# One of four weight sums of a Strassen-like gate/up unit, made by a load and an adding transfer instead of by GpSimd

## The chip, the cores and the metric

The kernel runs on one core of one Trainium2 chip. A core has TensorE (PE in the profile; PEld is its weight load), VectorE (DVE), ScalarE (ACT), GpSimd (POOL) and SyncE (SP), which here only issues DMA transfers. The metric is the device time of one execution in microseconds; runs of before and after are compared on the same chip.

## The reference, cut to what matters

The program is a decoder trunk of two layers on 512 tokens of width 1024, float32. Each layer has two SwiGLU FFNs with a mixer between them. The change touches the FFNs alone:

```python
def swiglu(h, w_gate, w_up, w_down):
    return (jax.nn.silu(h @ w_gate) * (h @ w_up)) @ w_down

for l in range(DEPTH):                       # 2
    x = x + 0.5 * swiglu(rms_norm(x, ffn1_norm[l]), ffn1_w_gate[l], ffn1_w_up[l], ffn1_w_down[l])
    ...                                      # mixer: convolution and differential attention
    x = x + 0.5 * swiglu(rms_norm(x, ffn2_norm[l]), ffn2_w_gate[l], ffn2_w_up[l], ffn2_w_down[l])
```

`w_gate` and `w_up` are 1024 x 2816, `w_down` is 2816 x 1024.

## The kernel before, in words

**Layout and precision.** Features lie on the 128 partitions, tokens along the row. D_FF is cut into 22 tiles of 128. Each float32 operand of a matmul is split in two float32r parts: a high part by a ScalarE copy and a low part, the operand less its high part, by VectorE. A product is then three matmuls (high x high, high x low, low x high).

**An FFN.** `ffn` does its first 5 feature tiles plainly (`PLAIN`), with three matmuls of 512 columns per step. The other 17 run as *units* in two parts, `PARTS[1:]`: 8 gate/up units and 4 Down units, then 9 gate/up units and 4 Down units. A gate/up unit makes the gate and the up product of one feature tile together as a 2 x 2 block product: two halves of the features by two halves of the tokens. With a Winograd form it needs seven half products in place of eight. Each half product is 4 steps of 3 matmuls of 256 columns, so a unit has 84 matmuls (L378, `product`).

**The weights of a unit.** With u1, u2 the first and second half of the up weights (128x512 each) and g1, g2 those of gate, the seven products need seven weight blocks. Four raw tiles hold them:

- A: u1 + u2, then u2 (A is the loaded up tile, its first half overwritten by the sum)
- B: g1, g2 (the loaded gate tile)
- C: g1 + u1 + u2, then g1 + g2 + u1 + u2
- D: g1 + u1, 128x512

`GateUp.load` (L456 on) loads u and g through SP's queue (L458, L459: 512 KB each), and `Unit.sums` makes the four sums on GpSimd: D (L355), A (L356) and the two halves of C (L357, L358). Then each of the four tiles is split by `hi` (ScalarE, L364) and `lo` (VectorE, L368).

**Buffers.** The raw tiles A, B and C come from a ring of 5 (`wraw`), D from a ring of one (`wraw2`). The high and low parts have rings of 4 for A, B, C and of 2 for D (`whi2`, `wlo2`). The two rings of 2 are used once more: by the two halves of the third plain tile of the first FFN (`by_halves`).

**The order of the work.** `Unit.body` writes the order of one unit: its products, the copies of partial sums out of PSUM (`keep`: L396, L407, L427), the finishing of the unit before, and the splits for the next unit. The matmuls that begin a half product are held in program order (L380). All other instructions are placed by a scheduler that simulates the program: it may move an instruction ahead on its engine as soon as what it needs is there, and each engine then runs its list strictly in order. In the body the order is: product with A (u1 + u2), copy `keep[3]` (L396), A of the next unit split, product with u2, B of the next unit's high part, the product with D of the unit *before* (`rest`), product with g1, copy `keep[:2]` (L407), D of the next unit split, product with g2, C of the next unit split, the two products with C, and copy `keep[2]` (L427).

**Neighbours.** In the mixer and at the ends of an FFN, `Prep` makes the next stage's operands: high part (L226, ScalarE), low part (L227, VectorE), square (L235, ScalarE) and its running sum on GpSimd (L239). TensorE transposes that sum (L196) and VectorE and GpSimd (L189) make the norm of each row from it. The Down units (`Down.load`, loads at L512) use the same `sums` with the same rings and keep it in the change.

Of the kernel before, what the change touches and what calls it, by code (L numbers as in the profile page):

```python
# [15 lines left out]
ALU = mybir.AluOpType  # L16
# [52 lines left out]
def trunk(ctx: ExitStack, tc: tile.TileContext, xt, par, lamv, relb, onehot,  # L69
          gu1, dn1, wag, wqkv, wout, gu2, dn2, out):  # L70
    nc = tc.nc
    V, S, G, T = nc.vector, nc.scalar, nc.gpsimd, nc.tensor
# [20 lines left out]
    def ring(tag, n=1024):  # L93
        dt = F32 if "raw" in tag else F32R
        return wp.tile([P, n], dt, tag=tag, name=tag, bufs=RING[tag])
# [70 lines left out]
    for k0, k1 in ((0, 1), (1, 4), (4, KT)):  # L166
        h = slice(k0 * P, k1 * P)
# [281 lines left out]
    class GateUp(Unit):  # L449
# [6 lines left out]
        def load(self):  # L456
            u, g = ring("wraw"), ring("wraw")
            nc.sync.dma_start(u, self.src[1])  # L458
            nc.sync.dma_start(g, self.src[0])  # L459
            d, more = ring("wraw2", 512), ring("wraw")  # L460
            h = slice(0, 512), slice(512, 1024)
            self.sums(u[:, h[0]], u[:, h[1]], g[:, h[0]], g[:, h[1]], d, more[:, h[0]], more[:, h[1]])
            self.raw = {"A": u, "B": g, "C": more, "D": d}
            self.cols = {k: n for k, (_, n) in self.WIDE.items()}

# [754 lines left out]
```

## Time and profile before

| what | us |
|---|---|
| median of 3 runs | 1781.65 |
| lowest, highest run | 1780.59, 1783.45 |
| the profiled execution, its own time | 1779.9 |
| its span in the profile | 1778.1 |
| GpSimd's D sums (L355): 68 of 128x512 in gate/up units | 95.2 busy |
| DMA traffic over the span | 177.87 MB, 100 GB/s |

The profile is of one execution. A row of the timeline reads: start, duration (us), engine, line, operation, written tile <- read tiles, shape; in brackets, how long the engine was idle before it and who released it. In a table of stretches, each engine has its busy time and its number of instructions. In the list of DMA issues the last number is the median time from the issue to the landing. The tile names `wraw`, `whi`, `wlo` stand for all rings, with D's among them: a 128x512 split at L364 or L368 is D's.

### The profile page before, as it was taken

How to read it: one execution, taken by the hardware profiler on the slowest of the kernel's cores; microseconds unless marked ns; L12 is line 12 of the kernel's file. 1: busy time of each engine (PE TensorE's matmuls, PEld its weight loads, DVE VectorE, ACT ScalarE, POOL GpSimd, SP SyncE). 2: the span in 40 equal slices, each digit the busy share in tenths (PEclk: the TensorE clock that was granted, in tenths of full speed). 3: DMA queues.
4: the chain of work that ended last, by engine and by line, in shares of the span. 5: the costliest groups of instructions: out<-in, count | busy, mean ns of one | idle time of the engine just before them, and what ended most of it. 6: DMA issues, size and time to landing. Idle time of an engine off the chain costs nothing.

```text
span 1778.1 us, 30234 instructions
## 1 busy us (share of the span) xinstructions
PE 1765.5 (99%) x11725; PEld 1617.3 (91%) x11725; DVE 1394.3 (78%) x1997; ACT 986.9 (56%) x1579; POOL 965.4 (54%) x665
## 2 busy tenths in 40 slices
PE   9999999999999999999999999999999999999999
PEld 7899999988788899999988999999877888999998
DVE  6978787868857978788767887877788588787875
ACT  6456565645844456466534664665558354564663
POOL 2276566379952156566303655653898433565661
PEclk9999999999999999999999999999999999999999
DMA  6233333423122223333332333334230232333332
GB/s 225 96 113 96 107 107 105 144 85 96 47 72 83 83 95 107 107 98 118 118 95 72 108 96 108 106 102 148 72 119 25 72 107 73 106 96 108 107 105 75
DMA packets 74225, 177.87 MB, mean 100 GB/s; under 512 B 8951, under 2 KB 30726, under 8 KB 74080
## 3 DMA queue, kind: packets, MB, share of 16 engines
q1 hardware_dynamic: 72480, 174.10, 31.1%
q8 instruction: 92, 1.51, 0.3%
q0 software_dynamic: 1312, 1.67, 0.3%
q14 instruction: 53, 0.43, 0.1%
q10 hardware_dynamic: 288, 0.16, 0.0%
HBM read 173.79 MB, written 3.42 MB: 100 GB/s over the span
## 4 chain that ended last, share of the span: by engine, by line
PE 89%; DVE 6%; issue 2%; POOL 2%; ACT 1%; DMA 0%; DVEq 0%; SPq 0%; ACTq 0%
PE ps_pair L378 48%; PE ps_pair L141 5%; PE ps_pair L142 5%; PE ps_pair L138 5%; PE ps_d L378 3%; DVE wlo L368 2%; PE ps_d L141 2%; PE ps_d L142 2%; PE ps_d L138 2%; PE ps_sc L990 2%; PE ps_pair L867 2%; PE ps_pair L868 2%; PE ps_pair L866 2%; PE ps_out L138 1%; PE ps_out L142 1%
## 5 line engine op out<-in xcount | busy, mean ns | idle before, releaser
L368 DVE TENSOR_TENSOR wlo<-wraw,whi 128x1024 fp32r<-128x1024 f32 (+4 forms) x400 | 510.3, 1277 | 171.9 <-ACT whi L364 171.4
L364 ACT ACTIVATE whi<-wraw 128x1024 fp32r<-128x1024 f32 (+4 forms) x400 | 373.6, 935 | 333.5 <-PE ps_pair L378 153.1
L355 POOL TENSOR_TENSOR wraw<-wraw 128x512 f32<-128x512 f32 (+1 forms) x100 | 127.8, 1278 | 554.7 <-DVE wlo L368 366.5
L378 PE MATMUL ps_pair<-acth,wlo 128*128 128x256 f32 x1088 | 307.9, 283 | 0.0
L378 PE MATMUL ps_pair<-actl,whi 128*128 128x256 f32 x1088 | 307.9, 283 | 0.0
L378 PE MATMUL ps_pair<-acth,whi 128*128 128x256 f32 x1088 | 307.9, 283 | 0.0
L378 PE MATMUL ps_pair<-th,whi 128*128 128x256 f32 x816 | 231.8, 284 | 1.2 <-ACT keep L427 0.4
L378 PE MATMUL ps_pair<-tl,whi 128*128 128x256 f32 x816 | 230.9, 283 | 0.0
L378 PE MATMUL ps_pair<-th,wlo 128*128 128x256 f32 x816 | 230.9, 283 | 0.0
L378 PEld LDWEIGHTS ps_pair<-actl,whi 128*128 128x128 f32 x1088 | 208.9, 192 | 0.2
L378 PEld LDWEIGHTS ps_pair<-acth,whi 128*128 128x128 f32 x1088 | 208.9, 192 | 0.2
L378 PEld LDWEIGHTS ps_pair<-acth,wlo 128*128 128x128 f32 x1088 | 208.9, 192 | 0.0
L101 ACT ACTIVATE whi<-wraw 128x1024 fp32r<-128x1024 f32 (+3 forms) x124 | 123.2, 1000 | 150.5 <-PE ps_pair L141 84.3
L141 PE MATMUL ps_pair<-actl,whi 128*128 128x512 f32 x448 | 174.6, 390 | 0.6 <-DVE actl L227 0.5
L142 PE MATMUL ps_pair<-acth,wlo 128*128 128x512 f32 x448 | 174.2, 390 | 0.0
L138 PE MATMUL ps_pair<-acth,whi 128*128 128x512 f32 x448 | 173.6, 393 | 0.1
L357 POOL TENSOR_TENSOR wraw<-wraw 128x512 f32<-128x512 f32 (+1 forms) x100 | 169.3, 1693 | 7.9
L358 POOL TENSOR_TENSOR wraw<-wraw 128x512 f32<-128x512 f32 (+1 forms) x100 | 164.3, 1643 | 7.8
L378 PEld LDWEIGHTS ps_pair<-th,whi 128*128 128x128 f32 x816 | 156.6, 192 | 3.1 <-ACT keep L427 3.1
L378 PEld LDWEIGHTS ps_pair<-th,wlo 128*128 128x128 f32 x816 | 156.6, 192 | 0.0
L378 PEld LDWEIGHTS ps_pair<-tl,whi 128*128 128x128 f32 x816 | 156.6, 192 | 0.0
L356 POOL TENSOR_TENSOR wraw<-wraw 128x512 f32<-128x512 f32 (+1 forms) x100 | 149.9, 1499 | 7.6
(203 smaller groups left out, 4402.1 us busy)
## 6 DMA issues: line engine op xcount, KB each, us to landing
wraw<-in_gu SPq DMA_DIRECT2D x172, 512.0 KB, 3.5
wraw<-in_wqkv SPq DMA_DIRECT2D x24, 512.0 KB, 3.5
wraw<-in_wag SPq DMA_DIRECT2D x16, 512.0 KB, 3.6
wraw<-in_wout SPq DMA_DIRECT2D x16, 512.0 KB, 3.5
wraw<-in_dn SPq DMA_DIRECT2D x60, 128.0 KB, 3.1
wraw<-in_dn SPq DMA_DIRECT2D x20, 384.0 KB, 3.2
wraw<-in_dn SPq DMA_DIRECT2D x28, 256.0 KB, 3.1
wraw<-in_dn SPq DMA_DIRECT2D x20, 320.0 KB, 3.5
```

The source lines that it names most:

```text
L101: S.activation(hi, raw, AF.Copy)
L138: first = T.matmul(ps, wh, xh, start=start, stop=False)
L141: T.matmul(ps, wh, xl, start=False, stop=False)
L142: T.matmul(ps, wl, xh, start=False, stop=stop)
L355: G.tensor_tensor(d, g1, u1, op=ALU.add)
L356: G.tensor_tensor(u1, u1, u2, op=ALU.add)
L357: G.tensor_tensor(m0, u1, g1, op=ALU.add)
L358: G.tensor_tensor(m1, m0, g2, op=ALU.add)
L364: pinned(S.activation(hi[:, : self.cols[k]], self.raw[k][:, : self.cols[k]], AF.Copy), pin)
L368: pinned(V.tensor_tensor(out=lo[:, :c], in0=self.raw[k][:, :c], in1=f32(hi[:, :c]), op=ALU.subtract), pin)
L378: mm = T.matmul(ps, l, r, start=first and i == n == 0, stop=False, skip_group_check=True)
L866: T.matmul(ps[n], xh[:, t], wh, start=k == 0, stop=False)
```

## The change

In `GateUp.load`, D is no longer summed on GpSimd. SP loads the first half of the gate weights into D's buffer, GpSimd does the three other sums, and GpSimd's DMA queue issues a transfer that adds the first half of the up weights, read from HBM once more, to D's buffer.

```diff
@@ -459,7 +459,11 @@
             nc.sync.dma_start(g, self.src[0])
             d, more = ring("wraw2", 512), ring("wraw")
             h = slice(0, 512), slice(512, 1024)
-            self.sums(u[:, h[0]], u[:, h[1]], g[:, h[0]], g[:, h[1]], d, more[:, h[0]], more[:, h[1]])
+            nc.sync.dma_start(d, self.src[0][:, h[0]])
+            G.tensor_tensor(u[:, h[0]], u[:, h[0]], u[:, h[1]], op=ALU.add)
+            G.tensor_tensor(more[:, h[0]], u[:, h[0]], g[:, h[0]], op=ALU.add)
+            G.tensor_tensor(more[:, h[1]], more[:, h[0]], g[:, h[1]], op=ALU.add)
+            nc.gpsimd.dma_start(d, self.src[1][:, h[0]], accum_op=ALU.add)
             self.raw = {"A": u, "B": g, "C": more, "D": d}
             self.cols = {k: n for k, (_, n) in self.WIDE.items()}
```

In the changed kernel the new lines are L462 (load of D), L463 (A sum), L464 and L465 (C sums) and L466 (adding transfer); every line behind them has a number higher by 4. Both transfers of a unit move 128 rows of 2 KB (256 KB).

## The prediction

> **What bounds the kernel now.** I read the page first (shares of the engines, then the chain), then the table of stretches, then TensorE's own waits, and last one gate/up unit in order of time.
>
> ```profile
> span 1778.1 us, 30234 instructions
> ...
> PE 1765.5 (99%) x11725; PEld 1617.3 (91%) x11725; DVE 1394.3 (78%) x1997; ACT 986.9 (56%) x1579; POOL 965.4 (54%) x665
> ...
> PE 89%; DVE 6%; issue 2%; POOL 2%; ACT 1%; DMA 0%; DVEq 0%; SPq 0%; ACTq 0%
> ```
>
> TensorE (PE) is busy in all but 12.6 us (1778.1 less 1765.5), and the chain runs along it. A change on GpSimd (POOL) can win no more than its share of these 12.6 us; it can lose any amount by making TensorE wait.
>
> ```profile
> 133.00:177.00 44.00, 44.00 (x369) 44.00 (x368) 38.15 (x55) 27.44 (x46) 27.24 (x19) 1.00 0.32 97
> ...
> 488.00:533.00 45.00, 42.66 (x255) 36.23 (x254) 24.73 (x73) 20.97 (x57) 26.07 (x20) 1.00 0.23 71
> ...
> 1733.00:1778.00 45.00, 40.75 (x275) 37.58 (x273) 23.55 (x30) 13.58 (x20) 6.97 (x6) 0.99 0.22 74
> ```
>
> Columns: stretch, length, then busy us of PE, PEld, DVE, ACT, POOL. The idle time lies at the end (4.3 us) and in the mixers (2.3 us in the second row). Among the units PE is full: 369 matmuls in 44 us are 0.119 us each, so a gate/up unit with 84 of them (7 products, 4 steps, 3 matmuls) lasts **10.0 us**. Of PE's waits only this one belongs to the units:
>
> ```profile
> PEld ps_pair L378 <- ACT keep L427: 3.1, 9, 0.6
> ```
>
> It comes about once in each of the eight unit parts. Here it is, with the neighbours that matter below, engine by engine:
>
> ```profile
> 126.50 0.33 SPq L458 DMA_DIRECT2D wraw<-in_gu  x1
> ...
> 126.62 0.68 DVE L368 TENSOR_TENSOR wlo<-wraw,whi 128x512 fp32r<-128x512 f32 x1
> ...
> 127.38 1.29 POOL L355 TENSOR_TENSOR wraw<-wraw 128x512 f32<-128x512 f32 x1 [5.10 <-DVE wlo L368]
> 128.75 2.16 POOL L356 TENSOR_TENSOR wraw<-wraw 128x512 f32<-128x512 f32 x1
> ...
> 130.94 1.06 ACT L364 ACTIVATE whi<-wraw 128x1024 fp32r<-128x1024 f32 x1 [1.94 <-POOL wraw L356]
> 131.91 0.36 ACT L427 ACTIVATE keep<-ps_pair 128x256 f32<-128x256 f32 x1
> ...
> 134.51 0.62 ACT L364 ACTIVATE whi<-wraw 128x512 fp32r<-128x512 f32 x1
> 135.50 0.60 ACT L407 ACTIVATE keep<-ps_pair 128x512 f32<-128x512 f32 x1 [0.37 <-PE ps_pair L378]
> ...
> 132.32 0.39 PE L378 MATMUL ps_pair<-th,whi 128*128 128x256 f32 x1
> ...
> 138.18 0.28 PE L378 MATMUL ps_pair<-th,whi 128*128 128x256 f32 x1
> ```
>
> D's low part of one unit ends at 127.30, which frees the only D buffer. GpSimd's sum for the next D follows, then its A sum (L356) to 130.91; the high part of A waits for it; the copy L427 stands behind that on ScalarE (ACT) until 132.27, and PE's next product begins at 132.32, some 0.3 us late.
>
> **The change part by part.** *Removed:* 68 sums of D on GpSimd (17 gate/up units in each of 4 FFNs), 1.3 us each in the row above. Because the A sum then waits for no D buffer, the high part of A can move ahead, and the wait for L427 goes: at most 3.1 us for nine, and as the ninth may lie elsewhere I take 8 x 0.3 = **-2.4 us**. What is late next is PE itself, so the rest of the 68 x 1.3 us is worth nothing. The Down units keep their four sums.
>
> *Added:* 68 loads of 256 KB on SP's queue and 68 adding transfers from GpSimd. In the order in which the changed kernel's instructions stand, D is no longer tied to its unit's sums. SP has, in the steady part, A of unit n+1, D of n, B of n+1; GpSimd has the A sum of n+1, the adding transfer for D of n, the two C sums of n+1. ScalarE and VectorE keep their order, apart from the first two D splits of each FFN, which come far earlier (below). The load waits until D of n-1 is split; so D becomes a ring of one buffer: load, add, high part, low part, next load. If one turn is longer than 10.0 us, it sets the pace of the gate/up units.
>
> ```profile
> wraw<-in_gu SPq DMA_DIRECT2D x172, 512.0 KB, 3.5
> ...
> wraw<-in_dn SPq DMA_DIRECT2D x60, 128.0 KB, 3.1
> ...
> wraw<-in_dn SPq DMA_DIRECT2D x28, 256.0 KB, 3.1
> ...
> d<-d POOLq DMA_DIRECT2D x1, 1280.0 KB, 19.3
> ...
> lamv<-in_lamv POOLq DMA_DIRECT2D x2, 128.0 KB, 3.2
> ...
> oneh<-in_onehot POOLq DMA_DIRECT2D x1, 66.0 KB, 4.4
> ```
>
> The turn without the add: the load is between the 256 KB and the 512 KB row, 3.3 us, since the A load was issued just ahead; four handovers of 0.08 us (127.30 to 127.38) are 0.3; high part 0.6, low part 0.7. Together 4.9 us, so 10.0 - 4.9 = **5.1 us remain for the add**, from issue to landing. The trace has no adding transfer. The bounds are GpSimd's own transfers: 3.2 us for half the bytes and no second read, and 19.3 us for five times the bytes between two places in HBM. I take **4.5 us**, nearest to the 3.2 us row: doubled bytes and the second read of D are each a doubling, worth 0 to 0.4 us by SP's three rows, and the B load beside it shares the DMA engines, for which I add the rest (the 66 KB row took 4.4 us, more than its bytes explain). So one turn is 9.4 us and fits, with 0.6 us to spare.
>
> There is a deadline inside the unit. ScalarE stands in order: the high part of D (134.51), then L407, whose copy PE needs before 138.18. L407 lasts 0.60, the high part 0.62, so D must land by about 136.9 or PE waits. D's load issued at 127.4 lands at 130.7; the A sum must end first (A's load of 126.50 lands at 130.0, the sum takes 1.3 to 2.2 us, to 131.4 to 132.2); the add lands 4.5 us later, **135.9 to 136.8**. In time, by 0.1 to 1.0 us. Then VectorE's low part is at most 2 us later than now; PE uses D only in the rest product of the following unit, and that begins (132.32 for the unit before) a whole unit later. SP's B load stands behind D's load, but waited for a later split (C) anyway; the C sums wait behind the add's issue on GpSimd, some 0.6 us in place of 1.3. These I cost at nothing; their cover is the 10 us of the unit.
>
> The transfer's issue needs GpSimd itself:
>
> ```profile
> 29.95 2.48 DVE L102 TENSOR_TENSOR wlo<-wraw,whi 128x1024 fp32r<-128x1024 f32 x2
> ...
> 31.29 0.59 POOL L764 DMA_DIRECT2D oneh<-in_onehot  x1
> ```
>
> An issue in the middle of VectorE's splits took 0.59 us, as elsewhere. The Trainium skill (SBUF — State Buffer, section "SBUF: two separate sides") warns that a VectorE instruction in a two-port mode locks GpSimd out, so that it can't write descriptors; its example goes from 0.62 to 3.1 us. By that rule an add behind one 1.2 us split would land at 5.7 us and the case would be the slower rival below; the row agrees that these two-input splits don't do it, as far as one issue can show.
>
> *Moved: the first D splits.* At the start they fall between other work with room. At the two ends of the first FFN of a layer they stand ahead of the next mixer's sum of squares:
>
> ```profile
> 332.96 1.20 DVE L368 TENSOR_TENSOR wlo<-wraw,whi 128x512 fp32r<-128x512 f32 x1
> ...
> 344.00 0.68 DVE L571 SCALAR_TENSOR_TENSOR x<-ps_pair,x 128x512 f32<-128x512 f32 x1
> ...
> 352.01 0.72 ACT L226 ACTIVATE acth<-x,par 128x512 fp32r<-128x512 f32 x1 [2.39 <-DVE x L571]
> ...
> 353.40 2.99 POOL L239 TENSOR_TENSOR ssum<-ssum,sq 128x512 f32<-128x512 f32 x2 [2.54 <-ACT sq L235]
> ...
> 357.17 0.60 PE L196 MATMUL ps_rows<-ident,ssum 128*128 128x128 f32 x4
> ```
>
> The first D of the second FFN can be loaded from 334.2 on, and is split behind L571, to 345.4. The second is loaded from there, lands at 348.7, is added by 353.2; its high part ends at 353.8, and L226, which now starts at 352.01, stands behind it: 1.8 us late. The squares and the sums L239 follow as late; they end at 356.39 now and PE's transposes L196, which are held in place, start at 357.17. So 0.8 us hide, and PE waits 1.0 to 1.1 us (the add's time less 3.4). Two such places: **+2.2 us**. At the end of each layer's second FFN the split stands ahead of the last x as well, but the sums have more room there; I take none.
>
> Sum against the profiled execution, 1779.9 us (span 1778.1 and 1.8 around it): -2.4 + 2.2 = -0.2, so 1779.7. The median of the runs, 1781.65, is 1.75 above the profiled time, which gives about **1781.5**.
>
> **The rivals.** *Slower: the ring of D is longer than the unit.* This decides from an add of 5.1 us on. At 6.0 us each turn is 10.9, and every gate/up unit behind the first slips by 0.9: in the part of 8 units D is made early for three, so 4 slips, in the part of 9 there are 8. That is 12 x 0.9 x 4 FFNs = 43 us, and 2 x 2.6 at the mixers: 1779.9 + 43 + 5 = 1828, with the 1.75 about 1830. At 5.5 us: 12 x 0.4 x 4 = 19 and 4, so 1805 at most, less what one unit's slack takes up. For it: the unmeasured add, with the room of 0.6 us; against it: all but the largest of GpSimd's own transfers landed in under 4.5 us. *Faster:* the wait on L427 goes, and a quick add (3.2 us) leaves the mixers alone: 1781.65 - 2.4 = 1779.2, still within 0.2% (3.6 us). More would have to come from the mixers' or the end's idle time, where nothing is removed; I give it little. *It doesn't do what it says:* the add does not stand behind its unit's sums but ahead of the next unit's C sums, and if the D load lands late GpSimd stands still with those sums behind it. They have some 8 us (C is split a unit later), so by itself this gives the forecast's time.
>
> A page gives a price: the Trainium skill (DMA: Bandwidth & Descriptors, section "Anatomy of one DMA — SWDGE (gpsimd) path") fits 2.0 us plus bytes at 436 GB/s, which for the two reads of 512 KB is an estimate of 3.2 us; by it the ring turns in 8.1 us and the sum is -2.4. No run here shows an adding transfer yet.
>
> **How the numbers follow.** Two tenths of a per cent, 3.6 us, is about what a measurement of this kernel can tell from no change. Forecast, no change: 0.50, with 1778 to 1785 as its own range. Slower by the ring: 0.45, a third of it beyond 1830. Faster by over 0.2%: 0.05. The range runs from 1778 to 1830 and leaves out some 0.2.
>
> **What would show it.** The adding transfer's row among the DMA issues: under 5.1 us to landing, forecast; over it, slower, with ScalarE's high part (128x512) waiting for a DMA and PE behind L407. The waits of PE on L427 gone, the A sum starting without VectorE. L196 starting about 1 us later against the matmuls ahead of it. I am wrong if PE waits in the gate/up units while the add lands early, or if TensorE gains more than 3 us there.

## The result, and the profile after

The changed kernel takes **1789.95 us** (median of 6 runs, 1785.45 to 1794.35), the kernel before, run beside it, 1781.33 (6 runs, 1780.59 to 1783.45): a ratio of 1.0047, 95% interval 1.0030 to 1.0064. The change costs about 8.6 us. A second series of the same kernel (below) gave more, 1.0086.

The page of the profiled execution (1787.99 us), its span, busy times and the shares of the chain:

```profile
span 1786.0 us, 30653 instructions
...
PE 1768.1 (99%) x11725; PEld 1619.2 (91%) x11725; DVE 1409.8 (79%) x1997; ACT 982.3 (55%) x1579; POOL 915.8 (51%) x665
...
PE 86%; DVE 5%; DMA 5%; ACT 2%; issue 1%; POOL 1%; SPq 0%; DVEq 0%; ACTq 0%; POOLq 0%
```

GpSimd does less (965.4 to 915.8 us), and that is worth nothing. TensorE's idle time grew from 12.6 to 17.9 us (1786.0 less 1768.1), its busy time by 2.6 us for the same 11725 matmuls, and DMA, which had no share of the chain, has 5%. Who TensorE waits for, from the list of waits:

```profile
PE ps_rows L196 <- POOL ssum L239: 4.1, 2, 2.9
...
PE ps_pair L378 <- ACT keep L427: 1.0, 3, 0.3
PE ps_bias L771 <- DMA oneh<-in_onehot: 0.8, 1, 0.8
...
PE ps_pair L378 <- ACT keep L407: 0.7, 1, 0.7
```

Where the time came from can be read place by place, since TensorE runs almost the same list in both kernels: I set the start of each matmul of the changed kernel against that of the matmul with the same number before, and summed the jumps of the difference.

| place | us |
|---|---|
| eight waits on L427 that are gone, 0.36 each | -2.9 |
| one more of them, near 1575 us | -0.6 |
| start, the wait for `oneh` | +0.8 |
| eleven places in the gate/up and Down units, 0.2 to 1.0 each | +4.5 |
| the two mixers' L196, 1.4 and 3.1 | +4.5 |
| a stretch of half TensorE clock, near 1335 us | +1.6 |

Together 7.9, which is the span's growth. Six of the eleven places, 2.6 us, are waits on L427 again, at other places than before: where a part goes over from gate/up to Down units (see "The deadline" below). The stretches that hold these places (PE's busy time is the second number, the granted clock stands third from the end):

```profile
133.00:177.00 44.00, 43.68 (x364) 43.48 (x363) 37.84 (x54) 27.13 (x45) 21.77 (x17) 1.00 0.47 129
266.00:311.00 45.00, 44.28 (x369) 44.08 (x368) 36.73 (x53) 27.80 (x46) 22.32 (x17) 1.00 0.49 143
355.00:400.00 45.00, 43.83 (x198) 36.04 (x197) 28.20 (x39) 23.05 (x33) 31.77 (x22) 1.00 0.36 121
...
1244.00:1289.00 45.00, 42.09 (x190) 34.58 (x190) 29.11 (x42) 23.25 (x34) 33.31 (x24) 1.00 0.29 95
1333.00:1378.00 45.00, 43.84 (x197) 33.03 (x198) 35.23 (x83) 34.29 (x73) 39.78 (x30) 0.96 0.11 36
```

The stretch of units that was full before (44.00 of 44) lacks 0.32 us now. In the third and fourth rows stand the mixers, in the last the lower clock.

The DMA issues, and with the line's own list the adding transfer's least, median and longest landing:

```profile
wraw<-in_gu SPq DMA_DIRECT2D x72, 256.0 KB, 3.2
wraw<-in_gu POOLq DMA_DIRECT2D x68, 256.0 KB, 4.3
...
L466 POOL DMA_DIRECT2D wraw<-in_gu x68: 848/872/969, 19.3 to 1715.0; - x68
...
DMA to landing us min/median/max: 3.6/4.3/7.8
```

So the unmeasured transfer lands in 4.3 us, under the forecast's 5.1, and yet the units wait. One turn of D's buffer shows how, at the place where TensorE loses most in a unit (timeline, all engines):

```profile
272.64 0.33 SPq L462 DMA_DIRECT2D wraw<-in_gu  x1
274.57 1.40 POOL L463 TENSOR_TENSOR wraw<-wraw 128x512 f32<-128x512 f32 x1 [2.51 <-DMA wraw<-in_gu]
276.38 0.86 POOL L466 DMA_DIRECT2D wraw<-in_gu  x1 [0.41 <-issue]
281.15 0.63 ACT L364 ACTIVATE whi<-wraw 128x512 fp32r<-128x512 f32 x1 [2.86 <-DMA wraw<-in_gu]
281.69 0.58 ACT L407 ACTIVATE keep<-ps_pair 128x512 f32<-128x512 f32 x1
281.82 0.69 DVE L368 TENSOR_TENSOR wlo<-wraw,whi 128x512 fp32r<-128x512 f32 x1 [2.09 <-ACT whi L364]
282.32 0.39 PE L378 MATMUL ps_pair<-th,whi 128*128 128x256 f32 x1 [0.71 <-ACT keep L407]
282.54 0.33 SPq L462 DMA_DIRECT2D wraw<-in_gu  x1
```

The load is issued at 272.64, the add at 276.38, the high part starts at 281.15, the low part ends at 282.51, and the next load follows in 0.03. That is 9.9 us, but the turn began late. The high part stands ahead of L407 on ScalarE; before, L407 waited 0.84 us for TensorE at this place, and now TensorE's next product waits 0.71 us for L407.

### The profile page after: what moved, and what is told of

Read it like the earlier page. It is cut to its first block, busy times and chain, and to the rows that moved or that the text cites. A ratio compares the mean times of both kernels' runs of the same rounds, so it can differ in the third digit from the quotient of the medians.

```text
span 1786.0 us, 30653 instructions
## 1 busy us (share of the span) xinstructions
PE 1768.1 (99%) x11725; PEld 1619.2 (91%) x11725; DVE 1409.8 (79%) x1997; ACT 982.3 (55%) x1579; POOL 915.8 (51%) x665
## 4 chain that ended last, share of the span: by engine, by line
PE 86%; DVE 5%; DMA 5%; ACT 2%; issue 1%; POOL 1%; SPq 0%; DVEq 0%; ACTq 0%; POOLq 0%
PE ps_pair L378 48%; PE ps_pair L141 5%; PE ps_pair L142 5%; PE ps_pair L138 5%; DMA wraw<-in_gu 4%; PE ps_d L378 3%; PE ps_d L138 2%; PE ps_d L141 2%; PE ps_d L142 2%; PE ps_sc L994 2%; PE ps_pair L871 2%; PE ps_pair L870 2%; PE ps_pair L872 2%; DVE wlo L368 1%; PE ps_out L138 1%
## 5 line engine op out<-in xcount | busy, mean ns | idle before, releaser
L368 DVE TENSOR_TENSOR wlo<-wraw,whi 128x1024 fp32r<-128x1024 f32 (+4 forms) x400 | 519.5, 1299 | 156.5 <-ACT whi L364 154.8
L463 POOL TENSOR_TENSOR wraw<-wraw 128x512 f32<-128x512 f32 x68 | 106.3, 1564 | 243.3 <-DMA wraw<-in_gu 109.7
L464 POOL TENSOR_TENSOR wraw<-wraw 128x512 f32<-128x512 f32 x68 | 119.1, 1752 | 152.0 <-DMA wraw<-in_gu 56.3
L378 PE MATMUL ps_pair<-hl,whi 128*128 128x256 f32 (+1 forms) x464 | 140.2, 302 | 0.0
L378 PE MATMUL ps_pair<-hh,whi 128*128 128x256 f32 (+1 forms) x464 | 140.1, 302 | 0.0
```

The costliest lines, as they stand in the source:

```text
L368: pinned(V.tensor_tensor(out=lo[:, :c], in0=self.raw[k][:, :c], in1=f32(hi[:, :c]), op=ALU.subtract), pin)
L378: mm = T.matmul(ps, l, r, start=first and i == n == 0, stop=False, skip_group_check=True)
L463: G.tensor_tensor(u[:, h[0]], u[:, h[0]], u[:, h[1]], op=ALU.add)
L464: G.tensor_tensor(more[:, h[0]], u[:, h[0]], g[:, h[0]], op=ALU.add)
```

## The experiments

Theory 1 was that D's one buffer is the cause: its turn uses up the unit, and D comes late. Theory 2 was that the early splits of the first D of each FFN cause the mixers' gaps, and that gaps let the clock drop. The rival was the traffic: 35.7 MB more, and 68 issues on GpSimd. Each ratio is to the kernel before in the same series (1781.73 us in the first four, 30 runs; 1781.45 in the last four, 23 runs).

**Two buffers for D.** Two allocations gave the room: the padding `SPACE` of another tile, and a tile of ones that a view of an equal one can stand for. The third and the sixth experiment use the same room.

```diff
-    RING = {..., "wraw2": 1, ...}
-SPACE = 392
-    ones = const.tile([P, P], F32, tag="ones", name="ones")
-    G.memset(ones, 1.0)
+    RING = {..., "wraw2": 2, ...}
+SPACE = 0
+    ones = f32(ones_r)
```

> Theory 1 (one buffer for D: its turn of load, add, high part and low part takes about 10.3 us, a unit 10.0, so D comes late and TensorE waits): with a second buffer the load of the next D waits for nothing, the 4.5 us that TensorE loses in the gate/up units of the changed kernel go, and ScalarE's wait of its high part (128x512) for the adding transfer, 92.7 us in 54 waits, falls under 20 us. In the two mixers the second D is added one turn earlier, so the waits of L196 (1.2 and 2.9 us) shrink too, and with them the drops of the granted clock. Time 1779 to 1783. Rival (the added traffic or GpSimd's issues are what costs, whatever waits for D): 1786 to 1790 as the changed kernel, granted clock 0.997 to 0.999.

Measured: **1777.87 us**, ratio 0.9975 (0.9965 to 0.9985). All the transfers are still there. ScalarE's waits for the adding transfer, TensorE's waits in the units and the wait of L196 are gone from the list. The same unit as above, ScalarE (this kernel's lines are one lower) and SP:

```profile
269.18 0.33 SPq L461 DMA_DIRECT2D wraw<-in_gu  x1
...
275.23 0.58 ACT L482 ACTIVATE keep<-ps_pair 128x512 f32<-128x512 f32 x1
275.71 0.63 ACT L363 ACTIVATE whi<-wraw 128x512 fp32r<-128x512 f32 x1
277.27 0.60 ACT L406 ACTIVATE keep<-ps_pair 128x512 f32<-128x512 f32 x1 [0.93 <-PE ps_pair L377]
```

The load goes out at 269.18 rather than 272.64, the high part starts without a wait, and L407 (here L406) again waits for TensorE, not the other way round. Theory 1 holds for the units, and the mixers go with it; the result lies a little below what I expected (1779).

**The first two D of each FFN summed on GpSimd**, the others by transfer.

```diff
+            if self.first:
+                self.sums(u[:, h[0]], u[:, h[1]], g[:, h[0]], g[:, h[1]], d, more[:, h[0]], more[:, h[1]])
+            else:
                 nc.sync.dma_start(d, self.src[0][:, h[0]])
                 ...
+            units[0].first = units[1].first = True
             units[0].load()
```

> Theory 2 (the early splits of the first two D of each FFN cost 0.8 us at the start and 1.4 and 3.1 us at the two mixers, and the long gaps there are what lets the granted clock drop): with GpSimd's sums for these two units alone, 64 transfers in place of 68, the waits of L196 of 4.1 us go, the clock comes back to 1.000, and only the 4.5 us of the units stay against the 2.9 us gained at L427: 1781 to 1784. Rival (the transfers of all units cost alike, by traffic): 1786 to 1790, clock 0.997 to 0.999.

Measured: 1786.31 us (1783.08 to 1789.11), ratio 1.0022 (1.0013 to 1.0031). The wait of L196 is gone, as theory 2 says. (The expectation's count of transfers is wrong: eight units are summed, so 60 adding transfers remain.) Two things are not as it says. The time is 2 us above its range, since the units lost 6.2 us in this execution, not 4.5. And the mean granted clock of the runs is 0.9984, not 1.000. But the kernel before has 0.9986 in this series, so with the mixers' gaps gone the clock is back where it was (the changed kernel has 0.9977).

**The traffic alone.** The kernel before with both transfers into a spare tile; a copy of two columns ties them to their unit.

```diff
             self.sums(u[:, h[0]], u[:, h[1]], g[:, h[0]], g[:, h[1]], d, more[:, h[0]], more[:, h[1]])
+            G.tensor_copy(spare[:, :2], d[:, :2])
+            nc.sync.dma_start(spare, self.src[0][:, h[0]])
+            nc.gpsimd.dma_start(spare, self.src[1][:, h[0]], accum_op=ALU.add)
```

> The kernel before with the two transfers of each unit added, into a tile that nothing reads; D is summed on GpSimd as before. Theories 1 and 2 (waiting for D costs, not the traffic): within 0.2% of the kernel before, 1780 to 1784, granted clock 1.000. Rival (traffic, or 0.87 us of issue on GpSimd per unit): most of the loss is here too, 1786 to 1790, clock 0.997 to 0.999, and loads of A and B that land later than 3.5 us.

Measured: 1779.39 us, ratio 0.9986 (0.9977 to 0.9995). The traffic is that of the change, the A and B loads land later (3.9 us median, before 3.5), as the rival said, and it costs nothing:

```profile
wraw<-in_gu SPq DMA_DIRECT2D x172, 512.0 KB, 3.9
spare<-in_gu SPq DMA_DIRECT2D x68, 256.0 KB, 3.0
spare<-in_gu POOLq DMA_DIRECT2D x68, 256.0 KB, 3.8
```

It is even a little faster than before: seven of the eight waits on L427 are gone here too, although the A sum still stands behind D's. They hang on a few tenths; at one of them the high part of A starts at 253.04 rather than 253.20. What brings these tenths was not followed.

**D summed last on GpSimd**, from C's first half, with no transfer.

```diff
-            self.sums(u[:, h[0]], u[:, h[1]], g[:, h[0]], g[:, h[1]], d, more[:, h[0]], more[:, h[1]])
+            G.tensor_tensor(u[:, h[0]], u[:, h[0]], u[:, h[1]], op=ALU.add)
+            G.tensor_tensor(more[:, h[0]], u[:, h[0]], g[:, h[0]], op=ALU.add)
+            G.tensor_tensor(more[:, h[1]], more[:, h[0]], g[:, h[1]], op=ALU.add)
+            G.tensor_tensor(d, more[:, h[0]], u[:, h[1]], op=ALU.subtract)
```

> The kernel before with D summed last of the four on GpSimd, as the difference of C's first half and u2, with no transfer added. Theory (the 2.9 us that the changed kernel gains in eight units come from the A sum no longer standing behind D's buffer, not from GpSimd having less to do): the same gain here, 1777.5 to 1779.5, no wait on L427. Rival (the wait moves to another sum): 1780 to 1782.

Measured: **1778.14 us**, ratio 0.9977 (0.9968 to 0.9986), no wait on L427. GpSimd's sums in one unit, in the new order (L465 is D, L462 is A):

```profile
249.96 1.30 POOL L465 TENSOR_TENSOR wraw<-wraw 128x512 f32<-128x512 f32 x1 [0.63 <-DVE wlo L368]
251.81 1.69 POOL L462 TENSOR_TENSOR wraw<-wraw 128x512 f32<-128x512 f32 x1 [0.55 <-DMA wraw<-in_gu]
256.12 1.94 POOL L463 TENSOR_TENSOR wraw<-wraw 128x512 f32<-128x512 f32 x1 [2.63 <-DMA wraw<-in_gu]
```

D still waits for VectorE's split, but the A sum behind it belongs to the next unit and waits only for its load.

**The load without the add**, with everything else as in the change. D is then the first half of the gate weights alone; the kernel leaves u1 out of it.

```diff
-            nc.gpsimd.dma_start(d, self.src[1][:, h[0]], accum_op=ALU.add)
```

> The changed kernel without the adding transfer: D is the first half of the gate weights alone (u1 is left out of it); the load, the single buffer, the order of ScalarE, VectorE, TensorE and SP are the changed kernel's. Theory 1 (the turn of the one buffer decides, and the add with its issue is 4.5 us of it): the turn falls from 10.3 to about 6 us, D is always early, and neither the units nor L196 wait: 1777 to 1780. Rival (the early splits themselves cost at the mixers, since they stand ahead of L226): L196 still waits 1 us or more at two places, 1780 to 1784.

Measured: 1778.96 us, ratio 0.9984 (0.9975 to 0.9992). Neither the units nor L196 wait. The early splits themselves cost nothing; they cost when the add is late, and one buffer has room for the load but not for the load and the add.

**Two buffers and the four sums on GpSimd**, with no transfer.

```diff
-    RING = {..., "wraw2": 1, ...}
+    RING = {..., "wraw2": 2, ...}
```

> The kernel before, with its four sums on GpSimd, and D's ring of two buffers; no transfer added. Theory (the gain of 2.9 us is the A sum's freedom from D's buffer, and neither the transfer nor GpSimd's saved 95 us has a part in it): the same 1777.5 to 1779 as with the two transfers and two buffers. Rival (the offload itself gains something): 1780 to 1782, at least 1 us above that kernel.

Measured: 1778.08 us, ratio 0.9979 (0.9970 to 0.9987). With D's buffer out of the way, sums on GpSimd and sums by transfer (0.9975 in the first experiment) are equal within the intervals. The offload shows no gain of its own.

**Later sums of squares.** The kernel before, with TensorE kept waiting at the two mixers by passes that change nothing.

```diff
+            if k == KT - 1 and self.gain == "mix_norm":
+                for _ in range(3):
+                    G.tensor_scalar(sq, sq, 1.0, None, op0=ALU.mult)
```

> The kernel before, with three more passes of GpSimd over the last squares ahead of the last sum (L239) at the two mixers, some 3.7 us, so that TensorE waits there about 2.9 us as in the changed kernel's second mixer; no transfer is added. Theory (gaps on TensorE, not the traffic, lower the granted clock): beside 2 x 2.9 us of waiting the mean granted clock falls by 0.0005 or more against the kernel before (its 30 runs have 0.9986), half-clock stretches of 3.4 us follow the gaps: 1787 to 1791. Rival (the clock falls by the traffic): 1786 to 1788 and the clock as before.

Measured: 1797.41 us, ratio 1.0089 (1.0076 to 1.0102); mean granted clock 0.9950 (before in this series 0.9987), with no transfer added. Stretches of 3.41 us around the first gap:

```profile
357.61:361.02 3.41, 0.03 (x1) 0.00 (x0) 0.00 (x0) 0.00 (x0) 3.24 (x3) 1.00 0.09 36
361.02:364.43 3.41, 2.97 (x9) 2.57 (x10) 1.03 (x3) 0.20 (x1) 1.23 (x2) 0.50 0.00 0
364.43:367.84 3.41, 3.41 (x16) 2.77 (x15) 0.00 (x0) 1.08 (x2) 0.19 (x1) 1.00 0.00 0
```

An idle stretch at clock 1.00 is followed by one at 0.50, and that by 1.00 again: 9 matmuls in it, 16 in the next. Gaps lower the clock without any added traffic. The time is above the range; the gaps came out at 3.8 us each (I wanted 2.9), and the order inside the mixers moved. In the profiled execution the two gaps (7.6 us) and four half-clock stretches (some 1.6 us each) make up 14 of the 15.5 us by which its span is longer; the rest isn't accounted for.

**The changed kernel again.**

> The changed kernel once more, for the spread of its losses from run to run. Theory 1: waits in the gate/up units of 4 to 7 us in other units than in the first profile, since the room is about nothing and the landing time varies; the waits of L196 at the same two places; 1785 to 1794. Rival (a fixed set of late places): the same units wait the same time, and the runs differ by the granted clock alone.

Measured: 1797.54 us (6 runs, 1789.74 to 1799.85), ratio 1.0086 (1.0070 to 1.0101): above the range. Its waits:

```profile
PE ps_rows L196 <- POOL ssum L239: 6.2, 2, 3.3
PE ps_pair L378 <- ACT keep L407: 2.0, 5, 0.8
...
PE ps_bias L771 <- DMA oneh<-in_onehot: 1.3, 1, 1.3
```

By the same count as above, its profiled execution (the longest of the six) loses 6.6 us in the units, partly at other places (1.0 and 0.8 us at 834 and 255 us, nothing near 282), 6.7 at the two mixers and more at the start, and the clock is halved more often, 0.994 in the mean. The waits on L427 at the first Down units are there again, 2.6 of the 6.6 us. So the late places inside the gate/up units are not a fixed set: with no room left, the spread of the landings seems to decide where TensorE waits.

## Why the prediction was wrong

**Bound, and what is removed: right.** TensorE bounds the kernel, GpSimd's saved time is worth nothing, and the wait on L427 goes at eight places, 0.36 us each (forecast 8 x 0.3). Two experiments, the sums in another order and the second buffer without transfers, bear out the reason that was given, the A sum's wait for D's buffer: with that removed in another way, the same time is won with no transfer. It is not the only way to win it, as the traffic alone showed.

**The add: right.** 4.5 us forecast, 4.3 median to landing; how the 4.5 was put together (the doubled bytes, the second read, the B load beside it) was not tried term by term. The estimate of 3.2 us by the Trainium skill (DMA: Bandwidth & Descriptors, section "Anatomy of one DMA — SWDGE (gpsimd) path") was low. The lock of GpSimd that the Trainium skill describes (SBUF — State Buffer, section "SBUF: two separate sides") did not show: 54 of the 68 issues ran beside one of VectorE's splits, and like the other 14 they took 0.87 us and landed in 4.3, in the median. That issue is longer than the 0.59 us of a plain transfer; its longest is 0.97.

**The ring: wrong, and this is the step that failed.** "Together 4.9 us, so 10.0 - 4.9 = 5.1 us remain for the add", and "one turn is 9.4 us and fits, with 0.6 us to spare". From the starts of L462, L466 and the 128x512 splits, 54 turns in a row of units last 9.1 to 12.0 us, 10.36 in the mean. The parts are 3.68 from load issue to add issue, 4.55 to the high part, 2.11 to the low part's end. Without the add that is 5.8, not 4.9, so 4.2 us remained. Of the 0.9 missing, some 0.3 lies ahead of the add: the load lands after 3.1 us in the mean, a little less than the 3.3 I took, but the add's issue starts 0.58 us after that landing (0.56 in the median), where I had put a handover at 0.08. The other 0.6 is the low part, which I took at 0.68 us, from one row, right behind the high part. Its group of 128x512 (VectorE's groups by shape; behind the first bar stand busy us and mean ns), in the changed kernel and before:

```profile
L368 DVE TENSOR_TENSOR wlo<-wraw,whi 128x512 fp32r<-128x512 f32 x84 | 85.4, 1017 | 45.9 <-ACT whi L364 45.5
```

```profile
L368 DVE TENSOR_TENSOR wlo<-wraw,whi 128x512 fp32r<-128x512 f32 x84 | 63.9, 761 | 8.6 <-ACT whi L364 8.6
```

It lasts 1.02 us now, before 0.76 in the mean, and starts on average 0.36 us after the high part's end, behind other work of VectorE. This was not new. In the trace of before, the 68 high and low parts of the gate/up D's take 2.31 us together in the mean, from the high part's start to the low part's end, because the low part starts 0.92 us after the high part. The high part to the very low part that I read at 126.62 stood there too:

```profile
124.83 0.62 ACT L364 ACTIVATE whi<-wraw 128x512 fp32r<-128x512 f32 x1
```

From 124.83 to the low part's end at 127.30 are 2.47 us, where I put 1.3 and a handover. I built the turn from single durations, without their spread and the queues they stand in.

**The deadline: wrong by the same step.** "In time, by 0.1 to 1.0 us" was one typical unit, against a landing that runs from 3.6 to 5.9 us in these turns (7.8 for the first of all, at the start). What I named as the sign of error came: TensorE waits in the units while the add lands early, 4.5 us in one execution and 6.6 in another. More than half of the 4.5, 2.6 us at six places, comes from the Down units' sums, which I costed at nothing: their D sum (L355) needs the same single buffer, and the D ahead of it gives it back late. It is the old wait on L427 at a new place. One of the six, engine by engine:

```profile
1044.54 1.01 POOL L355 TENSOR_TENSOR wraw<-wraw 128x384 f32<-128x384 f32 x1 [4.41 <-DVE wlo L368]
1045.63 1.89 POOL L356 TENSOR_TENSOR wraw<-wraw 128x384 f32<-128x384 f32 x1
1047.55 1.06 ACT L364 ACTIVATE whi<-wraw 128x1024 fp32r<-128x1024 f32 x1 [1.40 <-POOL wraw L356]
1048.52 0.36 ACT L427 ACTIVATE keep<-ps_pair 128x256 f32<-128x256 f32 x1
1048.93 0.39 PE L378 MATMUL ps_pair<-th,whi 128*128 128x256 f32 x1
```

Before, this D sum started at 1039.74, 4.8 us earlier, while TensorE was only 2.8 us ahead of the changed kernel; so the sum has lost 2.0 us against TensorE. The A sum behind it also lasts longer, 1.89 us in place of 1.02. With two buffers, or without the add, none of the six waits is left.

**The mixers: the mechanism right, the size half.** The chain was as forecast, L226 behind the second D's high part:

```profile
355.40 0.63 ACT L364 ACTIVATE whi<-wraw 128x512 fp32r<-128x512 f32 x1 [3.95 <-DMA wraw<-in_gu]
355.93 0.71 ACT L226 ACTIVATE acth<-x,par 128x512 fp32r<-128x512 f32 x1
...
357.31 2.96 POOL L239 TENSOR_TENSOR ssum<-ssum,sq 128x512 f32<-128x512 f32 x2 [4.63 <-ACT sq L235]
360.32 0.66 PE L196 MATMUL ps_rows<-ident,ssum 128*128 128x128 f32 x4 [1.17 <-POOL ssum L239]
...
1237.07 0.87 POOL L466 DMA_DIRECT2D wraw<-in_gu  x1 [2.56 <-DVE wlo L102]
1242.45 0.63 ACT L364 ACTIVATE whi<-wraw 128x512 fp32r<-128x512 f32 x1 [5.71 <-DMA wraw<-in_gu]
1247.35 0.66 PE L196 MATMUL ps_rows<-ident,ssum 128*128 128x128 f32 x4 [2.91 <-POOL ssum L239]
```

The first mixer waits 1.17 us (forecast 1.0 to 1.1). In the second the add is issued 4.1 us after its load, not 3.4, and needs 5.4 us, not 4.5, so TensorE waits 2.91. A chain of two transfers was costed at its median; each loss beyond the 0.8 us of cover is paid in full.

**The start: wrong, small.** I said the early splits fall "between other work with room". VectorE's splits now follow without a break, GpSimd's products L789 ahead of the first `oneh` take 3.84 us in place of 3.30 and start later, `oneh` is issued at 32.23 instead of 31.29, and TensorE waits 0.8 us. That the splits are what slows the products was not tried by itself.

**The clock: not in the forecast.** I added 1.75 us from the profiled execution to the median as a matter of form. It is about one half-clock stretch: of the 53 runs of before in the experiments, those at a mean granted clock of 1.000 took 1779.74 to 1780.31 us and those at 0.997 took 1784.05 to 1784.34. The changed kernel's runs have 0.9977 and 0.9967 in the mean, before 0.9986 and 0.9987 in the two series of experiments: 0.0009 to 0.0020 of 1785 us, some 1.6 to 3.6 us of the loss.

**The rivals.** The slower one, given 0.45, is what came, with the right place and the wrong trigger. It decided "from an add of 5.1 us on"; the add was shorter, the rest of the turn longer, and 0.36 us too much per turn gave 4.5 to 6.6 us over the kernel, not its 17 (12 x 0.36 x 4). The rival left open "what one unit's slack takes up", and that may well be most of it: from 199.83 to 282.54 eight turns take 82.7 us, 2.7 more than eight units, and TensorE waits 1.1 us there. "It doesn't do what it says" stood on the right order and gave the forecast's time, which it did not have.

## What to carry to other kernels

A buffer that is refilled once per unit has to be priced as a ring: every step of a turn with the queue it stands in, and with the longest landing, not the median; when the sum comes within a tenth of the unit's length, count it as late, or give the ring a second buffer first. When an engine off the critical path causes a wait, ask which instruction it stands behind before taking work from it: here a new order of four sums, or a second buffer, gained 0.2% with no offload, and the offload added nothing. Take a step's length from all its rows, from the first engine's start to the last one's end, not from one short row. Where TensorE waits for a microsecond or more, add the chance of a half-clock stretch to the wait.

## What the runs showed of the hardware

After a gap of TensorE of 1.81 us its clock was halved for one stretch of 3.41 us, which cost 1.6 us. The same gap, at the same place of the mixer, in the changed kernel and (last fence) before:

```profile
1331.52:1334.93 3.41, 1.60 (x11) 1.27 (x10) 0.96 (x2) 3.41 (x6) 3.41 (x3) 1.00 0.13 25
1334.93:1338.34 3.41, 3.41 (x9) 2.67 (x8) 3.27 (x5) 1.47 (x4) 3.41 (x3) 0.50 0.40 145
```

```profile
1323.52:1326.93 3.41, 1.95 (x13) 1.50 (x11) 1.52 (x3) 2.89 (x5) 3.41 (x3) 1.00 0.00 0
1326.93:1330.34 3.41, 3.06 (x13) 2.55 (x14) 2.45 (x4) 2.59 (x5) 3.41 (x3) 1.00 0.51 154
```

In each trace the changes of the clock lie whole multiples of 3.413 us apart, and the rows are cut along that grid. After, the gap lies wholly inside one stretch (busy 1.60 of 3.41) and the next is at 0.50; before, it straddles an edge (1.95) and nothing happens. The Trainium skill (TensorE: Matmul & The Clock Gate, section "What's actually happening") describes such a free-running window of 3413 ns, which agrees, and drops the clock after an idle window; here a window that was busy for 0.47 of its time was followed by half clock. What decides isn't settled, and the place of the gap in the window is not enough: with the later sums of squares the same gap, 1.80 us, lies wholly inside a stretch too (from 1337.23, busy 1.61 of 3.41), and the next stayed at 1.00. Near 495 us stretches that were busy for 0.54 to 0.59 of their time were followed by half clock in seven of these traces, and one of 0.59 in that of before was not, nor one of 0.49 in the changed kernel near 1245 us.
